# Mixer steps after quarters of a dense tile, early set-up loads, and block sums of the second channel weights on GpSimd

## The chip, the cores and the metric

The kernel runs on one core of a Trainium2 chip. A core has five engines that work at the same time and wait for one another by semaphores: TensorE (PE in the profile; its weight loads are PEld), VectorE (DVE), ScalarE (ACT), GpSimd (POOL) and SyncE (SP), which issues DMAs. The metric is device time in microseconds for one execution, the median of three runs. The profile is one more execution, taken with the hardware profiler.

## The reference

It is one layer of an encoder over 2048 tokens of width 1024, all in float32:

```
h = rmsnorm(x, norm_mix);  proj = h @ w_in
y_a = short_conv(...)       # gated convolution over 3 tokens
y_b = s5(...)               # complex diagonal state space, scan, GLU
y_c = sliding_window_attention(...)   # 4 query heads, 2 key heads, sinks
y_d = hgrn2(...)            # gated linear recurrence, 4 heads
x = x + rmsnorm_by_group([y_a, y_b, y_c, y_d]) @ w_out
x = x + square(relu(rmsnorm(x, norm_ffn) @ w_ff1)) @ w_ff2     # 1024 -> 4096 -> 1024
```

## The kernel before

**Precision.** A float32 operand is split into a high part (a copy in fp32r by ACT) and a low part (raw minus high, by DVE); a product is then three matmuls, high by high, high by low, low by high (`mm3`, L508). Every weight block is loaded raw (`wr`, by SP), split into `wh` (L105 or L1128) and `wl` (L111 or L1129), and used. This is the "dense" work.

**The mixer.** The tokens are worked in four blocks of 512. For each block, generators give the dense tiles: `attn_in` (4 tiles), `hgrn_in` (4), `conv_group` (6), `s5_in` (2), `hgrn_in2` (4). A dense tile (`proj_fm` or `tm_tile`) is 24 matmuls of 128x512 into one PSUM bank `mm`. Beside them run *tracks*: generators of the small work of the four groups (`attn`, `hgrn`, `conv_finish`, `s5_step`, and `s5_setup`, which makes the tables and operators of the state space once). `dense` (L1065) runs a generator of dense tiles, and after each of its yields calls `advance` (L1050), which adds each track's pace to its account and lets it go one step for every whole unit in it. `drain` runs what is left of a track to its end. A second generator can be given as `side`: `make_hT(b + 1)`, the normalised and transposed input of the next block, in PSUM bank `tr`, or `out_in`, the input of the output projection. After the mixer, `outp` is the output projection (L1024).

**The attention track** works on four tiles of 128 tokens for each block. For a tile: `norm` (squares, DVE and GpSimd), three transposes and their evacuation to `qT` and `kT` (L753 to L760), and for each of two key heads the scores, the softmax, the transposes of the probabilities (L810) and the products (L826).

**The set-up track** first issues eleven loads (L229 to L244), then transposes, exponentials and sines on [128, 8] tiles in many small DVE instructions (L223, among others, reads the loaded `ldt`), tables by doubling, and operators that go to DRAM. Its `yield`s come after pieces of this.

**The channel mixer.** Both matmuls are done in 2x2 blocks with seven products instead of eight. The first (`ff1`, L1276, all matmuls in `prod`, L1267) has two halves of the tokens (`hf`) with 16 steps `j` each, so 32 steps; a step is seven products of 12 matmuls. `prep_step` makes the sums of the input for half 0 ahead of the loop and for half 1 in steps 2, 5, 8 and 11 of half 0; the latter go to DRAM and come back by `from_dram` (L1210), called at step 0 of half 1 under high priority. The second matmul (L1397) needs block differences of `w_ff2`, which `w2_sums(k)` makes for k = 0 to 15, one in each step of half 1: two loads into `x_` and `y_`, four subtractions, two stores into `tt_d`. The tiles of `prep_step`, `from_dram`, `w2_sums` and the later `sr` loads share the tag `xt`, which has two buffers.

**Order.** Nobody writes the queues by hand. Each instruction has a priority, by default its place in the program; a block under `tc.high_priority()` is put ahead. A planner lays the instructions of each engine in a fixed order from priorities and its own estimate of when an instruction is ready; on the chip each engine then works through its queue in that order and waits where an operand is not there yet. So an instruction can stand in its queue far from its place in the program, and a wait holds everything behind it on that engine.

Of the kernel before, what the change touches and what calls it, by code (L numbers as in the profile page):

```python
# [59 lines left out]
def emit(ctx, tc, a):  # L60
# [150 lines left out]
    def s5_setup():  # L211
        with tc.tile_pool(name="st", bufs=1) as st:
# [31 lines left out]
            SY.dma_start(out=db.rearrange("p a b -> p (a b)"), in_=a["s5_d"].partition_broadcast(16))  # L244

            pt = psum_sx()
            PE.transpose(pt[:, 0:8], lam[:, 0, :], ident[0:8, 0:8])
# [269 lines left out]
    def proj_fm(c0):  # L517
        ws = fm_units(a["w_in"], c0)
        ps = psum_mm()
        for k in range(KD):  # L520
            wh, wl = ws[k // 4]
            mm3(ps, wh[:, k % 4, :], wl[:, k % 4, :], hh[:, k, :], hl[:, k, :], k == 0, k == KD - 1)
        return ps

# [3 lines left out]
    def tm_tile(ws, i):  # L528
        ps = psum_mm()
        sl = slice(i * P, (i + 1) * P)  # L530
        for k in range(KD):
            wh, wl = ws[k]
            mm3(ps, hh[:, k, sl], hl[:, k, sl], wh, wl, k == 0, k == KD - 1)
        return ps

# [3 lines left out]
    def conv_group(b):  # L539
        ya = []  # L540
        for ct in range(2):
            ph = proj_fm(ct * P)
            with tc.high_priority():
                z = mix.tile([P, TB + 2], F32, tag="cvz", name="cvz")
                S.activation(out=z[:, 2:], in_=ph, func=AF.Copy)
            yield
            pc = proj_fm(512 + ct * P)
            with tc.high_priority():
# [7 lines left out]
                st8["ztail", ct] = zp  # L556
            yield
            pb = proj_fm(256 + ct * P)
            with tc.high_priority():
# [6 lines left out]
            ya.append(ac)  # L566
            yield
        st8["ya", b] = ya
# [26 lines left out]
    def s5_in(b):  # L595
        for ct in range(2):
            ps = proj_fm(768 + ct * P)
# [5 lines left out]
            yield  # L603

# [96 lines left out]
    def attn_in(b):  # L701
        ws = tm_units(a["w_in"], 1024)
        lst = []
        for i in range(4):
            ti = b * 4 + i
            ps = tm_tile(ws, i)
# [6 lines left out]
            yield  # L713
        st8["attn", b] = lst

    def attn(b):
# [30 lines left out]

        nx = norm(0)
        yield
        for i in range(4):  # L750
            ti = b * 4 + i
            qn, va, vs_next, (va_prev, vs_prev) = nx
            pt = psum_mx()  # L753
            for c in range(3):
# [5 lines left out]
            V.tensor_scalar(out=kT[:, k0:k0 + P], in0=pt[:, 256:384], scalar1=kgain, scalar2=None, op0=ALU.mult)  # L760
            yield
            ya = mix.tile([P, GW], F32, tag="aty", name="aty")
            nks = [min(3, ti * 2 + e + 1) * 64 for e in range(2)]
            for kv in range(2):
# [24 lines left out]
                for e in range(2):  # L789
# [11 lines left out]
                    vvs.append(parts)  # L801
                if kv == 1 and i < 3:
                    nx = norm(i + 1)
# [12 lines left out]
                else:  # L816
                    S.activation(out=pTs[:, 0], in_=pT[:, 0:256].rearrange("p (e q) -> p e q", e=2), func=AF.Copy)
                    V.tensor_copy(out=pTs[0:64, 1], in_=pT[0:64, 256:512].rearrange("p (e q) -> p e q", e=2))
                yield
                for rp in range(2):  # L820
# [25 lines left out]
    def hgrn_in(b):  # L846
        mk = lambda nm, n: [mix.tile([P, 2, 256], F32, tag=nm, name=nm, bufs=n) for _ in range(2)]
        QP, KQ, Fg = mk("QP", 2), mk("KQ", 2), mk("Fg", 2)
        for ct in range(2):
            ps = proj_fm(1536 + ct * P)  # L850
# [3 lines left out]
            yield  # L854
            ps = proj_fm(1792 + ct * P)
            with tc.high_priority():
                for hf in range(2):
# [5 lines left out]
                                    op0=ALU.mult, op1=ALU.add)  # L863
            yield
        st8["hg", b] = (QP, KQ, Fg)

    def hgrn_in2(b):
        ws = tm_units(a["w_in"], 2048)
        vs, gs = [], []
        for i in range(4):  # L870
            ps = tm_tile(ws, i)
            v = mix.tile([P, GW], F32, tag="hv", name="hv", bufs=4)
# [6 lines left out]
            gs.append(g)  # L879
            yield  # L880
        st8["hv", b] = vs, gs
# [142 lines left out]
    def outp(b):  # L1024
        for nh in range(2):
            ns = slice(nh * 512, (nh + 1) * 512)
            ws = tm_units(a["w_out"], nh * 512)
            for i in range(4):
                ps = tm_tile(ws, i)
                xr = c1.tile([P, 512], F32, tag="xr", name="xr", bufs=2)  # L1030
                t0 = b * TB + i * P
                SY.dma_start(out=xr, in_=a["x"][t0:t0 + P, ns])
# [3 lines left out]
                yield  # L1036

# [8 lines left out]

    def track(gen, pace, key):
        tracks.append([gen, pace, 0.0, key])

    def advance():  # L1050
        for t_ in list(tracks):
            t_[2] += t_[1]
            while t_[2] >= 1.0:
                t_[2] -= 1.0
                if next(t_[0], "end") == "end":
                    tracks.remove(t_)
                    break

# [6 lines left out]
    def dense(g, side=None):  # L1065

        for _ in g:
            if side is not None:
                next(side, None)
            advance()  # L1070

    with first(-4000):
        run(make_hT(0))
    s5p = None
    for b in range(NB):
        dense(attn_in(b))
# [23 lines left out]
    for b in range(3):  # L1100
        g = outp(b)
        for _ in range(4):
            next(g)
# [118 lines left out]
    def w2_sums(k):  # L1222
        x_, y_ = (big.tile([P, D], F32, tag="xt", name="w2r", bufs=2) for _ in range(2))
        for h, t_ in enumerate((x_, y_)):
            SY.dma_start(out=t_, in_=a["w_ff2"][(2 * k + h) * P:(2 * k + h + 1) * P, :])
        b11, b12, b21, b22 = x_[:, 0:512], x_[:, 512:], y_[:, 0:512], y_[:, 512:]
        tsub(b11, b12, b11)
        tsub(b12, b22, b12)
        tsub(b22, b22, b11)
        tsub(b21, b21, b22)  # L1230
        for h, t_ in enumerate((x_, y_)):
            SY.dma_start(out=tt_d[h][k], in_=t_)

# [86 lines left out]
    for hf in range(2):  # L1320
        for j in range(NJ):
# [119 lines left out]
```

## Time and profile before

| | |
|---|---|
| median of 3 runs | 2346.17 us (2341.35 to 2346.51) |
| the profiled execution | 2343.7 us, its span 2341.6 us |
| mixer, with the output projection | 0 to about 1015 us of the span |
| first channel matmul | about 1019 to 1711 us |
| second channel matmul | about 1715 us to the end |
| mean granted TensorE clock | 0.987 |
| DMA | 381.35 MB, 163 GB/s over the span |

Stretches are read by the idle time of PE in them, and then by what ended that idle time. In a row of waits stand the engine and line that waited, what it waited for, the total in us, how often, and the longest. In a row of a queue stand the start, the time of the instruction, engine and line, the tiles written and read, and in brackets the idle time before it and its releaser.

### The profile page before, as it was taken

The page shows a single profiled execution, that of the slowest core. Times are in us where ns is not written, and L with a number is a line of the kernel's source. Part 1 is how long each engine was busy: PE and PEld are TensorE (multiplying, and loading weights), DVE is VectorE, ACT ScalarE, POOL GpSimd, SP SyncE. Part 2 cuts the span into 40 slices and gives each one's busy share as a digit, 9 for nine tenths or more (in the row PEclk, how much of TensorE's full clock was granted, in tenths as well). Part 3 has the DMA queues.
Part 4 walks back from the last instruction along what each step waited for, and adds up shares of the span by engine and source line. Part 5 has one row for each costly group of instructions (what it writes and reads, how often), then busy time and mean ns, then how long its engine had stood idle before and what let it go on. Part 6 is the DMA issues. An engine that isn't in the chain of part 4 may idle for free.

```text
span 2341.6 us, 32446 instructions
## 1 busy us (share of the span) xinstructions
PE 2227.5 (95%) x11460; PEld 1761.9 (75%) x11460; DVE 1433.2 (61%) x3008; ACT 949.8 (41%) x1902; POOL 163.2 (7%) x208
## 2 busy tenths in 40 slices
PE   7799999999999999989999999999999999999999
PEld 6577777777777777767777777777778888888887
DVE  5786786787677654676655666676653344344342
ACT  4234325435433433455555554544543233133121
POOL 0122212121211110000000000000000000000000
PEclk9899999999999999999999999999999999999999
DMA  6323333434432547636656577888674454355542
GB/s 182 92 78 97 104 102 118 118 101 125 124 111 85 163 155 224 216 129 193 194 158 191 173 222 255 273 266 267 204 238 151 155 192 140 118 190 180 183 148 99
DMA packets 393347, 381.35 MB, mean 163 GB/s; under 512 B 35968, under 2 KB 310496, under 8 KB 393184
## 3 DMA queue, kind: packets, MB, share of 16 engines
q1 hardware_dynamic: 393184, 379.27, 52.5%
q8 instruction: 90, 1.47, 0.3%
q14 instruction: 73, 0.60, 0.1%
HBM read 261.77 MB, written 116.40 MB: 161 GB/s over the span
## 4 chain that ended last, share of the span: by engine, by line
PE 67%; DVE 13%; DMA 9%; ACT 4%; issue 3%; POOL 2%; SPq 1%; DVEq 0%; POOLq 0%; ACTq 0%
PE mm L1397 26%; PE mm L1267 10%; PE mm L509 5%; PE mm L511 5%; PE mm L510 5%; PE hx L1267 5%; DMA w2r<-in_w_ff_dram 2%; DVE wl L111 2%; PE mx L1267 2%; DVE tp L1138 2%; PE hx L921 1%; DMA fxs<-x1d 1%; PE mx L826 1%; ACT wh L1128 1%; DVE w2r L1138 1%
## 5 line engine op out<-in xcount | busy, mean ns | idle before, releaser
L1397 PE MATMUL mm<-wh,st 128*128 128x512 f32 x1792 | 561.8, 394 | 1.4 <-ACT wh L1128 1.4
L1397 PEld LDWEIGHTS mm<-wh,st 128*128 128x128 f32 x1792 | 337.4, 188 | 80.0 <-ACT wh L1128 1.9
L1397 PE MATMUL mm<-wl,st 128*128 128x512 f32 x896 | 353.6, 395 | 0.2 <-DVE wl L1129 0.2
L1267 PE MATMUL mm<-tb,wh 128*128 128x512 f32 x1024 | 330.3, 403 | 24.5 <-ACT tp L1280 6.5
L1368 ACT ACTIVATE st<-sr 128x1024 fp32r<-128x1024 f32 x112 | 114.6, 1054 | 402.8 <-PE mm L1397 359.2
L1267 PEld LDWEIGHTS mm<-tb,wh 128*128 128x128 f32 x1024 | 189.6, 191 | 85.1 <-ACT tp L1286 14.7
L105 ACT ACTIVATE wh<-wr 128x512 fp32r<-128x512 f32 x224 | 138.6, 628 | 201.8 <-PE mm L510 163.0
L509 PE MATMUL mm<-wh,hh 128*128 128x512 f32 x512 | 208.3, 407 | 2.1 <-ACT hh L504 2.1
L1129 DVE TENSOR_TENSOR wl<-wr,wh 128x512 fp32r<-128x512 f32 x208 | 138.1, 688 | 113.6 <-ACT wh L1128 70.2
L1267 PE MATMUL mm<-tb,wl 128*128 128x512 f32 x512 | 204.5, 399 | 0.0
L511 PE MATMUL mm<-wh,hl 128*128 128x512 f32 x512 | 204.4, 399 | 0.0
L510 PE MATMUL mm<-wl,hh 128*128 128x512 f32 x512 | 204.0, 398 | 0.0
L1397 PEld LDWEIGHTS mm<-wl,st 128*128 128x128 f32 x896 | 168.4, 188 | 40.5 <-DVE wl L1129 0.5
L1369 DVE TENSOR_TENSOR st<-sr,st 128x1024 fp32r<-128x1024 f32 x112 | 133.9, 1222 | 94.8 <-ACT st L1368 94.6
L1267 PE MATMUL hx<-tb,wh 128*128 128x512 f32 x512 | 162.3, 397 | 8.4 <-ACT wh L1128 8.4
L111 DVE TENSOR_TENSOR wl<-wr,wh 128x512 fp32r<-128x512 f32 x224 | 151.3, 694 | 30.5 <-ACT wh L105 26.3
L509 PE MATMUL mm<-hh,wh 128*128 128x512 f32 x384 | 159.5, 415 | 0.0
L511 PE MATMUL mm<-hh,wl 128*128 128x512 f32 x384 | 154.9, 403 | 0.0
L510 PE MATMUL mm<-hl,wh 128*128 128x512 f32 x384 | 154.5, 402 | 0.0
L1128 ACT ACTIVATE wh<-wr 128x512 fp32r<-128x512 f32 x208 | 125.4, 625 | 64.6 <-PE mm L1267 28.1
L1138 DVE TENSOR_TENSOR tq<-mm,tq 128x512 f32<-128x512 f32 x32 | 22.1, 691 | 173.0 <-PE mm L1397 172.9
L1273 ACT ACTIVATE tp<-tp 128x512 f32<-128x512 f32 x96 | 60.5, 630 | 163.0 <-DVE tp L1138 156.2
(372 smaller groups left out, 3627.6 us busy)
## 6 DMA issues: line engine op xcount, KB each, us to landing
as<-tp SPq DMA_DIRECT2D x224, 256.0 KB, 2.8
sr<-as SPq DMA_DIRECT2D x112, 512.0 KB, 4.4
wr<-in_w_ff_dram SPq DMA_DIRECT2D x176, 256.0 KB, 3.8
wr<-in_w_in_dram SPq DMA_DIRECT2D x160, 256.0 KB, 3.1
wr<-in_w_out_dram SPq DMA_DIRECT2D x64, 256.0 KB, 4.1
w2r<-in_w_ff_dram SPq DMA_DIRECT2D x32, 512.0 KB, 4.6
tt<-w2r SPq DMA_DIRECT2D x32, 512.0 KB, 2.7
wr<-tt SPq DMA_DIRECT2D x64, 256.0 KB, 4.0
```

The costliest lines, as they stand in the source:

```text
L105: S.activation(out=hi, in_=raw, func=AF.Copy)
L111: (G if le == "p" else V).tensor_tensor(out=lo, in0=raw, in1=hi, op=ALU.subtract)
L509: PE.matmul(ps, lhsT=lh, rhs=rh, start=first, stop=False)
L510: PE.matmul(ps, lhsT=lh, rhs=rl, start=False, stop=False)
L511: PE.matmul(ps, lhsT=ll, rhs=rh, start=False, stop=last)
L1128: S.activation(out=h, in_=raw, func=AF.Copy)
L1129: V.tensor_tensor(out=l, in0=raw, in1=h, op=ALU.subtract)
L1138: V.tensor_tensor(out=o, in0=x, in1=y, op=op)
L1267: PE.matmul(ps, lhsT=(wh, wl)[lw][:, ks], rhs=b[lb][:, k, :], start=first and k == 0 and q == 0, stop=k == 3 and q == 2, skip_group_check= ...
L1368: S.activation(out=s_[:, 0, ks], in_=r, func=AF.Copy)
L1369: V.tensor_tensor(out=s_[:, 1, ks], in0=r, in1=s_[:, 0, ks], op=ALU.subtract)
L1397: PE.matmul(ps, lhsT=st_[:, ls, k, :], rhs=tu[i, k][lt], start=k == 0 and p_ == 0, stop=k == NJ - 1 and p_ == 2)
```

## The change

- A dense tile yields after its second, fourth and sixth of its eight groups of three matmuls too (so after each 6 of its 24 matmuls), and `True` at its end. `dense` advances the tracks at each of these, and `side` at the ends alone. `advance` lets a track go one step at most. The paces are given anew: attention 1.35 per tile to 0.29 per quarter, set-up 1.5 to 0.45, HGRN 1.25 to 0.34, conv 0.5 to 0.15, S5 1.0 to 0.34 in block 2 and 0.27 in block 3; tracks begin with something in their account. The first half of `outp` advances by quarters as well.
- `s5_setup` yields after its loads. It is run up to there ahead of the first dense tile, and becomes a track after `hgrn_in(0)` instead of after `attn_in(0)`.
- In the attention, the transposes for the next tile (`turn`) are issued with the second key head of the tile before, in PSUM bank `tr` instead of `mx`; `norm` of the next tile comes with the first key head instead of the second.
- `w2_sums` has its DMAs issued by GpSimd instead of SP and its subtractions done by GpSimd instead of DVE. It is called in steps 12 to 15 of half 0 and 2 to 13 of half 1, instead of 0 to 15 of half 1.

```diff
@@ s5_setup, after its loads
+            yield
             pt = psum_sx()
@@ proj_fm, and the same in tm_tile
             mm3(ps, wh[:, k % 4, :], wl[:, k % 4, :], hh[:, k, :], hl[:, k, :], k == 0, k == KD - 1)
+            if k in (1, 3, 5):
+                yield
         return ps
@@ conv_group, and the same in s5_in, attn_in, hgrn_in, hgrn_in2 and outp
-            ph = proj_fm(ct * P)
+            ph = yield from proj_fm(ct * P)
...
-            yield
+            yield True
@@ attn
-        nx = norm(0)
-        yield
-        for i in range(4):
-            ti = b * 4 + i
-            qn, va, vs_next, (va_prev, vs_prev) = nx
-            pt = psum_mx()
+        def turn(i, qn):
+            pt = psum_tr()
...
             V.tensor_scalar(out=kT[:, k0:k0 + P], in0=pt[:, 256:384], scalar1=kgain, scalar2=None, op0=ALU.mult)
-            yield
+            return qT
+
+        nx = norm(0)
+        yield
+        qT_next = turn(0, nx[0])
+        yield
+        for i in range(4):
+            ti = b * 4 + i
+            _, va, vs_next, (va_prev, vs_prev) = nx
+            qT = qT_next
...
-                if kv == 1 and i < 3:
+                if kv == 0 and i < 3:
                     nx = norm(i + 1)
                 yield
...
+                if kv == 1 and i < 3:
+                    qT_next = turn(i + 1, nx[0])
                 yield
@@ advance
             t_[2] += t_[1]
-            while t_[2] >= 1.0:
+            if t_[2] >= 1.0:
                 t_[2] -= 1.0
                 if next(t_[0], "end") == "end":
                     tracks.remove(t_)
-                    break
@@ dense
-        for _ in g:
-            if side is not None:
+        for end in g:
+            if end and side is not None:
                 next(side, None)
             advance()
@@ the blocks
+    setup = s5_setup()
+    next(setup)
     for b in range(NB):
         dense(attn_in(b))
         drain("hg")
-        track(attn(b), 1.35, "at")
-        if b == 0:
-            track(s5_setup(), 1.5, "set")
+        track(attn(b), 0.29, "at", 0.5)
         if b == 2:
...
-            track(s5_step(0), 1.0, "s5")
+            track(s5_step(0), 0.34, "s5", 0.3)
         if b == 3:
...
-            track(s5_step(1), 1.0, "s5")
+            track(s5_step(1), 0.27, "s5", 0.3)
         dense(hgrn_in(b))
-        track(hgrn(b), 1.25, "hg")
+        if b == 0:
+            track(setup, 0.45, "set", 0.3)
+        track(hgrn(b), 0.34, "hg", 0.9)
         dense(conv_group(b))
-        track(conv_finish(b), 0.5, "cv")
+        track(conv_finish(b), 0.15, "cv")
@@ the output projection
-        for _ in range(4):
+        for n in range(16):
             next(g)
             advance()
@@ w2_sums
-            SY.dma_start(out=t_, in_=a["w_ff2"][(2 * k + h) * P:(2 * k + h + 1) * P, :])
+            G.dma_start(out=t_, in_=a["w_ff2"][(2 * k + h) * P:(2 * k + h + 1) * P, :])
...
-        tsub(b11, b12, b11)
-        tsub(b12, b22, b12)
-        tsub(b22, b22, b11)
-        tsub(b21, b21, b22)
+        for o, p_, q_ in ((b11, b12, b11), (b12, b22, b12), (b22, b22, b11), (b21, b21, b22)):
+            G.tensor_tensor(out=o, in0=p_, in1=q_, op=ALU.subtract)
...
-            SY.dma_start(out=tt_d[h][k], in_=t_)
+            G.dma_start(out=tt_d[h][k], in_=t_)
@@ the loop over steps of the first channel matmul
-            if hf == 1:
-                w2_sums(j)
+            n = hf * NJ + j
+            if 12 <= n < 16 or 18 <= n < 30:
+                w2_sums(n - 12 if n < 16 else n - 14)
```

More of the change, by code (lines that the diff above doesn't have):

```diff
@@ L533, in tm_tile @@
             mm3(ps, hh[:, k, sl], hl[:, k, sl], wh, wl, k == 0, k == KD - 1)
+            if k in (1, 3, 5):
+                yield
         return ps
@@ L545, in conv_group @@
                 S.activation(out=z[:, 2:], in_=ph, func=AF.Copy)
-            yield
-            pc = proj_fm(512 + ct * P)
+            yield True
+            pc = yield from proj_fm(512 + ct * P)
             with tc.high_priority():
@@ L556, in conv_group @@
                 st8["ztail", ct] = zp
-            yield
-            pb = proj_fm(256 + ct * P)
+            yield True
+            pb = yield from proj_fm(256 + ct * P)
             with tc.high_priority():
@@ L566, in conv_group @@
             ya.append(ac)
-            yield
+            yield True
         st8["ya", b] = ya
@@ L596, in s5_in @@
         for ct in range(2):
-            ps = proj_fm(768 + ct * P)
+            ps = yield from proj_fm(768 + ct * P)
             with tc.high_priority():
@@ L602, in s5_in @@
             SY.dma_start(out=u_d[b // 2][ct * P:(ct + 1) * P, :, n0:n0 + 64], in_=us)
-            yield
+            yield True
     def s5_step(s):
@@ L705, in attn_in @@
             ti = b * 4 + i
-            ps = tm_tile(ws, i)
+            ps = yield from tm_tile(ws, i)
             qk = mix.tile([P, 384], F32, tag="qk", name="qk", bufs=4)
@@ L712, in attn_in @@
             lst.append((qk, va))
-            yield
+            yield True
         st8["attn", b] = lst
@@ L746, in norm @@
             return qn, va, vs_next, prev
-        nx = norm(0)
-        yield
-        for i in range(4):
-            ti = b * 4 + i
-            qn, va, vs_next, (va_prev, vs_prev) = nx
-            pt = psum_mx()
+        def turn(i, qn):
+            pt = psum_tr()
             for c in range(3):
@@ L760, in attn @@
             V.tensor_scalar(out=kT[:, k0:k0 + P], in0=pt[:, 256:384], scalar1=kgain, scalar2=None, op0=ALU.mult)
-            yield
+            return qT
+        nx = norm(0)
+        yield
+        qT_next = turn(0, nx[0])
+        yield
+        for i in range(4):
+            ti = b * 4 + i
+            _, va, vs_next, (va_prev, vs_prev) = nx
+            qT = qT_next
             ya = mix.tile([P, GW], F32, tag="aty", name="aty")
@@ L849, in hgrn_in @@
         for ct in range(2):
-            ps = proj_fm(1536 + ct * P)
+            ps = yield from proj_fm(1536 + ct * P)
             with tc.high_priority():
@@ L853, in hgrn_in @@
                     S.activation(out=QP[hf][:, ct], in_=ps[:, hf * 256:(hf + 1) * 256], func=AF.Copy)
-            yield
-            ps = proj_fm(1792 + ct * P)
+            yield True
+            ps = yield from proj_fm(1792 + ct * P)
             with tc.high_priority():
@@ L863, in hgrn_in @@
                                     op0=ALU.mult, op1=ALU.add)
-            yield
+            yield True
         st8["hg", b] = (QP, KQ, Fg)
@@ L870, in hgrn_in2 @@
         for i in range(4):
-            ps = tm_tile(ws, i)
+            ps = yield from tm_tile(ws, i)
             v = mix.tile([P, GW], F32, tag="hv", name="hv", bufs=4)
@@ L879, in hgrn_in2 @@
             gs.append(g)
-            yield
+            yield True
         st8["hv", b] = vs, gs
@@ L1028, in outp @@
             for i in range(4):
-                ps = tm_tile(ws, i)
+                ps = yield from tm_tile(ws, i)
                 xr = c1.tile([P, 512], F32, tag="xr", name="xr", bufs=2)
@@ L1035, in outp @@
                 SY.dma_start(out=x1_d[b][i * P:(i + 1) * P, ns], in_=xr)
-                yield
+                yield True
     def run(g):
@@ L1045, in emit, with track @@
     tracks = []
-    def track(gen, pace, key):
-        tracks.append([gen, pace, 0.0, key])
+    def track(gen, pace, key, start=0.0):
+        tracks.append([gen, pace, start, key])
     def advance():
```

## The prediction

> **What bounds the kernel now.** I read the page first, then the table of stretches, then the waits of each engine inside the stretches, then the queues in order of time. TensorE (PE) is the bound nearly everywhere: the page gives it 95% of the span. The stretches show where it isn't. Columns: stretch, its length, busy time (and instructions) of PE, weight loads, DVE, ACT, POOL, granted clock, DMA share, GB/s.
>
> ```profile
> span 2341.6 us, 32446 instructions
> ...
> PE 2227.5 (95%) x11460; PEld 1761.9 (75%) x11460; DVE 1433.2 (61%) x3008; ACT 949.8 (41%) x1902; POOL 163.2 (7%) x208
> ...
> 45.00:65.00 20.00, 14.49 (x67) 11.15 (x65) 6.96 (x26) 5.46 (x13) 0.00 (x0) 0.93 0.51 119
> 65.00:245.00 180.00, 163.53 (x1125) 127.24 (x1126) 141.90 (x488) 69.56 (x190) 34.81 (x41) 0.94 0.33 96
> 245.00:430.00 185.00, 179.14 (x1220) 139.28 (x1219) 136.49 (x355) 73.03 (x198) 38.70 (x44) 1.00 0.37 104
> 430.00:605.00 175.00, 168.47 (x1224) 132.68 (x1223) 138.11 (x406) 70.25 (x199) 32.25 (x39) 1.00 0.39 111
> 605.00:790.00 185.00, 175.27 (x1165) 136.76 (x1164) 139.01 (x389) 74.84 (x214) 31.64 (x40) 0.97 0.40 116
> 790.00:965.00 175.00, 166.82 (x852) 135.26 (x853) 96.51 (x215) 63.26 (x143) 13.53 (x20) 0.99 0.59 193
> 1730.00:2341.00 611.00, 607.62 (x2615) 491.92 (x2614) 244.65 (x293) 166.94 (x212) 0.00 (x0) 1.00 0.48 158
> ```
>
> The last row is the second channel matmul, which has no idle PE to win and which the change leaves alone. The four rows from 65 to 790 are about one mixer block each. PE is idle for 16.5, 5.9, 6.5 and 9.7 us in them, and 5.5 us in the 20 us ahead. So block 0 (45 to 245) idles 22.0 us against a mean of 7.4 in the others. The cause stands in the waits of PE and in the queues of SP and DVE.
>
> ```profile
> PE mx L770 <- DVE kT L760: 8.6, 1, 8.6
> PE mx L810 <- DVE apr L790: 7.2, 4, 2.9
> ...
> 32.41 0.94 SPq L199 DMA_DIRECT2D wgr<-in_s_w_glu_dram  x2
> 33.40 0.52 SPq L727 DMA_DIRECT2D vs<-va  x1
> 33.96 0.52 SPq L229 DMA_DIRECT2D lam<-in_s_lam_re_dram  x1
> 43.11 4.14 SPq L102 DMA_DIRECT2D wr<-in_w_in_dram  x6
> ...
> 49.54 1.80 SPq L240 DMA_DIRECT2D ldt<-in_s_log_dt_dram  x2
> ...
> 61.73 0.17 DVE L223 TENSOR_SCALAR t<-ldt 128x8 f32<-128x8 f32 x1 [11.41 <-DMA ldt<-in_s_log_dt_dram]
> ```
>
> DVE stands 11.41 us at L223 for the load of `ldt`, and the attention's `kT` (L760) is queued behind it, so PE stands 8.6 us. The clock then falls:
>
> ```profile
> 62.40:72.60 10.20, 4.01 (x11) 3.21 (x12) 8.83 (x47) 3.88 (x8) 1.34 (x1) 0.50 0.63 209
> 79.40:89.60 10.20, 9.86 (x34) 7.23 (x35) 5.48 (x28) 2.20 (x10) 0.00 (x0) 0.50 0.18 52
> ```
>
> In those two stretches PE worked 4.01 + 9.86 us at half clock, of which half, 6.9 us, is lost. [...]
>
> The second place is the first channel matmul (L1267). Its 32 steps (16 for each half of the tokens) need 84 matmuls each. Rows of L1267 alone: stretch, length, PE busy, weight loads, clock, DMA.
>
> ```profile
> 1280.90:1320.70 39.80, 39.58 (x169) 31.20 (x170) 1.00 0.67 197
> 1413.10:1687.80 274.70, 262.99 (x1093) 203.69 (x1092) 0.99 0.81 258
> ```
>
> Two quiet steps of the first half take 39.8 us, 19.9 each. Thirteen steps of the second half, beside `w2_sums`, take 274.7, 21.13 each: 16.0 us more than thirteen quiet ones. From 1405 to 1715 the waits of DVE and SP name `w2_sums`:
>
> ```profile
> DVE w2r L1138 <- DMA w2r<-in_w_ff_dram: 31.7, 18, 3.7
> SPq L1232 <- DVE w2r L1138: 53.4, 26, 5.2
> SPq L1225 <- DMA tt<-w2r: 17.8, 12, 4.1
> ACT wh L1128 <- DVE tp L1138: 46.2, 14, 5.7
> ```
>
> **The change, part by part.** The sum is made against the profiled execution's own time, 2343.7 us (its span is 2341.6); the median of the runs shown, 2346.17, is 2.5 above.
>
> *Set-up loads and set-up track.* The eleven DMAs of the set-up are written ahead of the first dense tile, its arithmetic now starts after `hgrn_in(0)` instead of after `attn_in(0)`. At most this wins block 0's extra idle (22.0 - 7.4 = 14.6) and the half clock (6.9), 21.5 us. At least it wins nothing: in the queue the set-up loads already follow the last constant (L199, then one `vs` copy, then L229), so there is hardly an earlier place, and `ldt` comes 16 us after L229 because weights' loads (six in the L102 row) are put in between. What the move does remove is the crowd behind the wait: DVE was busy 8.83 of 10.20 us after it, mostly with set-up instructions, and the second wait (L810) and second half clock come from that. The order in the queues is not program order (priority decides, and what is ready fills gaps: `outp(0)`'s first load starts at 67 us), so L223 may still be put ahead of its data. The first `vs` copy now stands behind the set-up loads, eleven issues of about half a us (the L229 row); only the attention's products wait for it, later, and dense matmuls cover that. I take half, **11 us**.
>
> ```profile
> 67.31 0.97 SPq L1032 DMA_DIRECT2D xr<-in_x_dram  x2
> ```
>
> *Quarters.* No instruction is added. A track step now comes after a quarter of a dense tile (6 matmuls) instead of after 24, and never two at once. Attention goes from 1.35 steps a tile to 0.29 a quarter, 1.16 a tile, with 19 steps instead of 22, so it ends at the same place; HGRN 1.25 to 1.36; set-up 1.5 to 1.8; S5 1.0 to 1.36 in block 2. That last one matters: 25 steps at 1.0 a tile over 20 tiles left five for `drain("s5")`, run in one lump; at 1.36 none is left. The attention's transposes of the next tile go ahead of the last product, so `kT` is early. What can go is idle time in blocks 1 to 3, 5.9 + 6.5 + 9.7 = 22.1 us; the largest wait of 430 to 605 is only 2.3 us in three (the L810 row below), and much of the rest is dependence that stays. Against it: `turn` moves from the two `mx` banks to the single `tr` bank, which `make_hT` and `conv_finish` use too. If each of the 16 turns waited for one evacuation of that bank (0.60 us, the row below), 10 us would be lost. Between 22 won and 10 lost I take **7 us** won, a third of the idle, because the waits are many and short. The stretch 790 to 965 keeps its `out_in` at tile ends (the L1016 row): 0; half of its 5.8 us either way goes into the range.
>
> ```profile
> PE mx L810 <- DVE apr L790: 2.3, 3, 1.4
> PE tr L1016 <- DVE hl L1021: 5.8, 6, 2.0
> ...
> L504 ACT ACTIVATE hh<-tr 128x512 fp32r<-128x512 f32 x8 | 4.8, 600 | 1.3 <-PE tr L500 1.3
> ```
>
> *`w2_sums` on GpSimd.* From DVE go 64 subtractions of 0.691 us, 44.2, and the waits of 31.7; from SP's queue go 64 DMAs and the three waits on them (53.4 and 17.8 are the largest), behind which the weights' loads stood; ACT's weight splits (`wh`) stood 46.2 us behind DVE. GpSimd gets 64 subtractions and 64 DMAs; no pow is left for it after step 11, so nothing is queued behind them. The nearest GpSimd row is L904, 128x512 with two inputs; the two rows of `w2r` stand ahead of it:
>
> ```profile
> L1138 DVE TENSOR_TENSOR w2r<-w2r x64: 680/691/694, 1399.8 to 1653.7; 128x512 f32<-128x512 f32 x64
> DMA to landing us min/median/max: 2.6/3.6/6.7
> ...
> L904 POOL TENSOR_TENSOR hacc<-ident,he x16: 1037/1090/1557, 97.6 to 694.3; 128x512 f32<-128x512 f32 x16
> L939 POOL TENSOR_TENSOR KQ<-KQ,bp x48: 616/706/1667, 121.7 to 801.7; 128x256 f32<-128x256 f32 x48
> L842 DVE SCALAR_TENSOR_TENSOR goy<-aty,gorsc,g_grp x16: 475/485/1075, 106.5 to 787.4; 128x256 f32<-128x256 f32 x16
> ```
>
> Four of 1.09 are 4.4 us of a 19.9 us step, so GpSimd is not short of time. But the maxima beside the minima (1667 against 616 on GpSimd, 1075 against 475 on DVE) show that the two engines stop each other at times. The bound: every GpSimd subtraction stops DVE for its whole length, 64 x 1.09 = 69.8 us, against 44.2 + 31.7 = 75.9 freed. So at worst nearly all is given back, and at best the 16.0 us of the thirteen steps are won. DVE is two thirds busy there, so about half the meetings should hurt: I take **8 us**. [...]
>
> No row shows a DMA issued by GpSimd. The bounds: as cheap as SP's (the L1032 row: 0.97 us for two); at most, a step's four together cost one more landing, 6.7 us at worst for `w2r`. I take the first, since four DMAs a step fit in the time GpSimd has left; both ends are in rival 3. [...]
>
> Sum: 11 + 7 + 8 = 26; 2343.7 - 26 = 2317.7, and with 2.5 to the median **2320**.
>
> **The rivals.**
>
> 1. *The orders do not matter, because the loads are not early and the tracks already filled the gaps.* For it: L229 stands right behind the constants, and work is placed by readiness. Against it: the lump of five S5 steps and the double steps of attention and HGRN go, whatever else stays. Then only the 8 us of `w2_sums` remain: 2346 - 8 = 2338.
>
> 2. *The two engines exclude each other.* Then 69.8 of 75.9 us come back and `w2_sums` wins about 0; 2346 - 18 = 2328. Against it: only the maxima, not the medians, are long in the rows above.
>
> 3. *Slower: `from_dram` comes late.* `w2_sums(0..3)` now stand at steps 12 to 15, ahead of `from_dram`, and share the two `xt` buffers with it.
>
> ```profile
> L1216 SPq DMA_DIRECT2D tr<-tb x14: 320/338/555, 1277.5 to 1392.3; - x14
> L1218 DVE TENSOR_TENSOR tb<-tr,tb x14: 1218/1226/1227, 1333.8 to 1397.5; 128x1024 fp32r<-128x1024 f32 x14
> tt<-w2r SPq DMA_DIRECT2D x32, 512.0 KB, 2.7
> ```
>
> The last row is the store of a sum. Seven operands pass two buffers, each pair about a landing (5 us) and splits (2 us), 49 us. They end now at 1398.7. If four sums of t us each start at 1277.5, they end at 1277.5 + 4t + 49, later than now once t is over 18.0. By the rows t is 3.6 + 4 x 1.09 + a store of 2.7 = 10.7, and with every maximum 6.7 + 4 x 1.56 + 2.7 = 15.6; with 6.7 more for GpSimd's DMAs it is 22.3, and PE waits 17 us. With no gain in the mixer and 8 us of the later sums kept: 2346 + 17 - 8 = 2355.
>
> 4. *The mixer gets worse*: the 10 us of the `tr` bank, no set-up gain, half of `w2_sums`' 8: 2352.
>
> **How the numbers follow.** Forecast (2300 to 2337): 0.55. Rival 1: 0.16, rival 2: 0.12, rival 3: 0.10, rival 4: 0.07. The likeliest time is 2320. All upper bounds together, 21.5 + 22.1 + 16, would be 2286, which I hold for very unlikely; the range goes from 2298 to rival 3's 2354. No change means within 0.3%, 7 us, about what a measurement tells. Faster by more: the forecast, rival 2 and half of rival 1 (its 2338 lies on the edge), less 0.02 for sizes, 0.73. Within: the other half and 0.05 of rival 4, 0.13. Slower: rival 3, the rest of rival 4 and 0.02 for sizes, 0.14.
>
> **What would show it.** Right: DVE's wait on `ldt` short or gone, no half clock from 62 to 90, and PE idle in block 0 near 10; idle in blocks 1 to 3 near 15 together; steps of the second half near 20.5 us, DVE's wait on `w2r` gone. Wrong: L223 still at 61 us; PE waiting on `tr` for the attention's transposes; DVE's tensor_tensor median well over 0.69 beside GpSimd; `from_dram`'s splits ending after 1400.

## The result, and the profile after

The changed kernel takes **2378.73 us** in the median (2370.92 to 2381.45, 4 runs), the kernel before beside it 2346.34. The ratio is 1.013 (95% interval 1.0102 to 1.0158): 1.3% slower, where 2320 was predicted. The profiled execution of the changed kernel took 2370.92 us.

These lines are from the profile page of the changed kernel: the span, then the busy time of each engine. PE has exactly the busy time it had before; what was added is idle PE. POOL went from 163 to 293 us.

```profile
span 2369.2 us, 32494 instructions
...
PE 2227.5 (94%) x11460; PEld 1761.7 (74%) x11460; DVE 1429.9 (60%) x2944; ACT 952.5 (40%) x1902; POOL 293.1 (12%) x336
```

The mixer's stretches, in the columns of the first table of the prediction:

```profile
45.00:65.00 20.00, 12.39 (x54) 9.92 (x53) 7.04 (x23) 6.08 (x13) 1.22 (x1) 0.88 0.57 140
65.00:245.00 180.00, 168.09 (x1140) 129.33 (x1140) 142.82 (x486) 69.73 (x189) 37.27 (x42) 0.93 0.31 92
245.00:430.00 185.00, 177.00 (x1206) 137.46 (x1204) 136.89 (x354) 72.97 (x196) 36.18 (x43) 0.99 0.36 102
430.00:605.00 175.00, 164.60 (x1186) 126.77 (x1185) 141.22 (x414) 72.83 (x209) 33.72 (x41) 1.00 0.42 120
605.00:790.00 185.00, 178.56 (x1291) 140.51 (x1290) 145.52 (x402) 75.54 (x216) 34.93 (x42) 1.00 0.38 111
```

Block 0 idles 7.6 + 11.9 = 19.5 us (before 22.0), blocks 1 to 3 idle 8.0 + 10.4 + 6.4 = 24.8 (before 22.1). So there is no less idle time. The waits of 45 to 65 show that the wait of block 0 is still there:

```profile
DVE t L223 <- DMA ldt<-in_s_log_dt_dram: 10.3, 1, 10.3
...
PE mx L780 <- DVE kT L761: 7.6, 1, 7.6
```

The loss lies in the first channel matmul. Its matmuls alone (L1267 before, L1278 after): the whole, then step 14, steps 15 to 23, step 24, and steps 25 to 30. First the kernel before, then the changed one.

```profile
1019.40:1711.30 691.90, 648.01 (x2688) 501.38 (x2687) 0.99 0.69 212
1320.70:1344.60 23.90, 20.36 (x85) 15.32 (x83) 1.00 0.53 158
1344.60:1540.20 195.60, 184.32 (x757) 141.59 (x758) 0.98 0.80 251
1540.20:1564.50 24.30, 21.45 (x86) 16.51 (x85) 0.93 0.90 284
1564.50:1687.80 123.30, 119.34 (x505) 93.22 (x504) 1.00 0.78 247
```

```profile
1012.60:1739.70 727.10, 654.95 (x2688) 509.19 (x2687) 0.96 0.66 202
1317.10:1350.60 33.50, 23.28 (x86) 17.49 (x84) 0.80 0.73 229
1350.60:1561.80 211.20, 189.23 (x757) 145.86 (x758) 0.95 0.78 243
1561.80:1598.80 37.00, 21.98 (x85) 17.00 (x84) 0.82 0.77 247
1598.80:1716.30 117.50, 117.50 (x506) 93.73 (x505) 1.00 0.51 150
```

It is 35.2 us longer: steps 14 and 24 lose 9.6 and 12.7, the nine between them 15.6, and the six after the last sum, now at 19.6 each without any idle time, win 5.8. The rest is step 13 (19.57 us before, 23.63 after) and trifles. The second channel matmul is unchanged (630 us).

*The two long steps.* The waits of SP's queue, from 1310 to 1350 and from 1550 to 1600:

```profile
SPq L1229 <- DMA w2r<-in_w_ff_dram: 11.2, 1, 11.2
SPq L1229 <- DMA tt<-w2r: 9.4, 2, 8.2
```
```profile
SPq L1379 <- DMA w2r<-in_w_ff_dram: 21.8, 1, 21.8
SPq L1379 <- DMA tt<-w2r: 9.2, 2, 7.8
```

L1229 is the first `tr` load of `from_dram`, L1379 the first `sr` load of the second channel matmul. Both need one of the two `xt` buffers, which GpSimd's sums hold. Behind them, in the same queue, stand weights' loads in step 14 and, in step 24, the stores of `as` that set free the `tp` tiles. In the same two windows DVE, ACT and PE wait for those:

```profile
DVE tp L1151 <- DMA wr<-in_w_ff_dram: 7.7, 1, 7.7
...
PE hx L1278 <- ACT wh L1141: 6.6, 1, 6.6
```
```profile
ACT tp L1284 <- DMA as<-tp: 15.0, 1, 15.0
...
PE mm L1278 <- ACT tp L1284: 14.1, 1, 14.1
```

In these stalls the clock falls to half, for 13.7 and 13.6 us (the clock is the column before the last two):

```profile
1333.30:1347.00 13.70, 6.90 (x15) 4.96 (x16) 8.47 (x12) 4.25 (x8) 0.00 (x0) 0.50 1.06 328
...
1575.70:1589.30 13.60, 4.33 (x10) 3.47 (x11) 1.39 (x2) 1.23 (x2) 2.49 (x4) 0.50 0.89 281
```

*DVE beside GpSimd.* Groups of 1260 to 1600 (count, busy time, mean ns of one, then idle time before):

```profile
L1241 POOL TENSOR_TENSOR w2r<-w2r 128x512 f32<-128x512 f32 x64 | 91.0, 1421 | 61.0 <-DMA w2r<-in_w_ff_dram 59.4
...
L1142 DVE TENSOR_TENSOR wl<-tp,wh 128x512 fp32r<-128x512 f32 x56 | 43.9, 844 | 1.1 <-ACT wh L1141 1.1
L1151 DVE TENSOR_TENSOR tp<-tp 128x512 f32<-128x512 f32 x56 | 43.6, 814 | 30.0 <-ACT tp L1285 29.4
...
L1151 DVE TENSOR_TENSOR tp<-mx,tp 128x512 f32<-128x512 f32 x14 | 9.5, 680 | 0.0
L1151 DVE TENSOR_TENSOR tp<-hx,tp 128x512 f32<-128x512 f32 x13 | 9.0, 691 | 15.2 <-PE hx L1278 15.2
```

DVE's subtractions with two inputs in SBUF (`wl`, `tp<-tp`) went from 0.69 us to a mean of 0.81 to 0.84; those with one input in PSUM (`mx`, `hx`) stayed at 0.68 to 0.69. Single ones took up to 2.26 us; 33 were lengthened, by some 31.5 us together, and each of the 33 overlaps a subtraction of GpSimd. Fourteen subtractions with a PSUM input overlap GpSimd's too, and none of them took over 0.69 us.

### The profile page after: what moved, and what is told of

It is laid out like the page before. It is cut to its first block, busy times and chain, and to the rows that moved or that the text cites. A ratio compares the mean times of both kernels' runs of the same rounds, so it can differ in the third digit from the quotient of the medians.

```text
span 2369.2 us, 32494 instructions
## 1 busy us (share of the span) xinstructions
PE 2227.5 (94%) x11460; PEld 1761.7 (74%) x11460; DVE 1429.9 (60%) x2944; ACT 952.5 (40%) x1902; POOL 293.1 (12%) x336
## 4 chain that ended last, share of the span: by engine, by line
PE 60%; DMA 13%; DVE 12%; issue 6%; POOL 5%; ACT 4%; SPq 0%; POOLq 0%; DVEq 0%; ACTq 0%
PE mm L1409 25%; PE mm L1278 8%; PE mm L510 5%; PE mm L511 4%; PE mm L512 4%; DMA w2r<-in_w_ff_dram 4%; PE hx L1278 4%; POOL w2r L1241 3%; DMA tt<-w2r 2%; DVE wl L111 2%; PE mx L1278 2%; DMA fxs<-x1d 1%; PE hx L933 1%; DMA xt<-in_x_dram 1%; PE mx L838 1%
## 5 line engine op out<-in xcount | busy, mean ns | idle before, releaser
L1278 PE MATMUL mm<-tb,wh 128*128 128x512 f32 x1024 | 335.1, 408 | 39.6 <-ACT tp L1284 17.7
L1278 PEld LDWEIGHTS mm<-tb,wh 128*128 128x128 f32 x1024 | 193.8, 194 | 99.8 <-ACT tp L1284 23.4
L1142 DVE TENSOR_TENSOR wl<-wr,wh 128x512 fp32r<-128x512 f32 x208 | 145.0, 720 | 146.0 <-ACT wh L1141 76.6
L1278 PE MATMUL mm<-tb,wl 128*128 128x512 f32 x512 | 206.6, 404 | 0.0
L1278 PE MATMUL hx<-tb,wh 128*128 128x512 f32 x512 | 163.5, 399 | 11.6 <-ACT wh L1141 11.6
L111 DVE TENSOR_TENSOR wl<-wr,wh 128x512 fp32r<-128x512 f32 x224 | 151.2, 691 | 29.0 <-ACT wh L105 28.3
L1151 DVE TENSOR_TENSOR tp<-tp 128x512 f32<-128x512 f32 x136 | 96.1, 741 | 51.1 <-ACT tp L1285 49.2
```

What stands on the lines that cost most here:

```text
L111: (G if le == "p" else V).tensor_tensor(out=lo, in0=raw, in1=hi, op=ALU.subtract)
L1142: V.tensor_tensor(out=l, in0=raw, in1=h, op=ALU.subtract)
L1151: V.tensor_tensor(out=o, in0=x, in1=y, op=op)
L1278: PE.matmul(ps, lhsT=(wh, wl)[lw][:, ks], rhs=b[lb][:, k, :], start=first and k == 0 and q == 0, stop=k == 3 and q == 2, skip_group_check= ...
```

## The experiments

Three theories follow from these rows: **Q**, SP's queue stands behind the `xt` buffers; **L**, DVE and GpSimd stop each other; **M**, the mixer's new order matters. A fourth came with the first results: **P**, pace, that on GpSimd's queue nothing keeps the sums from running ahead and crowding the weights' work. Every ratio is to the kernel before on the same chip, with its 95% interval. The column "x clock" is the mean over a kernel's runs of span times mean granted clock, an estimate of what its time would be without half clock. It is a rough one: where PE waits anyway, half clock costs nothing (in the two stalls above PE worked 6.90 of 13.7 us and 4.33 of 13.6), so it comes out too low for kernels with such stalls. The kernel before has 2311.8 to 2313.4 in the five groups of runs, at clock 0.986 to 0.987.

| kernel | mixer | sums: buffers, arithmetic, DMAs, steps | median us | ratio | clock, x clock |
|---|---|---|---|---|---|
| changed | new | xt, GpSimd, GpSimd, 12-15 and 18-29 | 2378.7 | 1.0130 [1.0102, 1.0158] | .977, 2321.1 |
| mixer_only | new | as before | 2345.0 | 0.9999 [0.9984, 1.0014] | .984, 2303.4 |
| own_buffers | new | own, GpSimd, GpSimd | 2360.5 | 1.0064 [1.0044, 1.0084] | .980, 2310.2 |
| xt_dve_sub | new | xt, DVE, GpSimd | 2376.5 | 1.0136 [1.0119, 1.0153] | .978, 2320.8 |
| own_dve_sub | new | own, DVE, GpSimd | 2374.6 | 1.0118 [1.0097, 1.0140] | .976, 2314.0 |
| own_sp_dve | new | own, DVE, SP, 16-31 | 2342.0 | 0.9995 [0.9973, 1.0018] | .984, 2302.7 |
| own_sp_steps | new | own, DVE, SP, 12-15 and 18-29 | 2345.8 | 1.0001 [0.9982, 1.0020] | .982, 2303.0 |
| own_paced | new | own, GpSimd, GpSimd, held to 13-28 | 2336.6 | 0.9964 [0.9944, 0.9985] | .983, 2295.1 |
| own_dve_paced | new | own, DVE, GpSimd, held to 13-28 | 2347.4 | 0.9988 [0.9965, 1.0010] | .984, 2306.2 |
| xt_paced | new | xt, GpSimd, GpSimd, held to 13-28 | 2351.3 | 1.0021 [1.0003, 1.0039] | .982, 2307.7 |
| ff2_sums | new | second channel matmul, DVE, SP | 2386.7 | 1.0177 [1.0143, 1.0211] | .973, 2318.4 |
| ldt_first | new, `ldt` loaded first | as before | 2339.4 | 0.9979 [0.9957, 1.0001] | .984, 2302.4 |
| setup_held | new, loads held back | as before | 2345.1 | 0.9996 [0.9977, 1.0015] | .984, 2305.5 |
| best | new, loads held back | own, GpSimd, held to 12, 13, 17-30 | 2333.2 | 0.9937 [0.9908, 0.9965] | .985, 2295.8 |
| before_paced | before | as best | 2332.9 | 0.9940 [0.9915, 0.9964] | .988, 2304.0 |
| setup_only | before, set-up early | as best | 2337.5 | 0.9964 [0.9945, 0.9983] | .985, 2301.0 |
| quarters_only | quarters, set-up as before | as best | 2329.6 | 0.9942 [0.9918, 0.9966] | .985, 2294.2 |

**One part at a time: mixer, buffers, engine.** In `mixer_only`, `w2_sums` and its call are those of the kernel before. The others keep the changed kernel's calls. The own buffers are one `gain` and two `xr` tiles, idle by then; `xt_dve_sub` keeps `xt` and has only the last edit:

```
     def w2_sums(k):
-        x_, y_ = (big.tile([P, D], F32, tag="xt", name="w2r", bufs=2) for _ in range(2))
+        x_ = c1.tile([P, D], F32, tag="gain", name="w2r")
+        b21, b22 = (c1.tile([P, 512], F32, tag="xr", name="w2y", bufs=2) for _ in range(2))
...
-            G.tensor_tensor(out=o, in0=p_, in1=q_, op=ALU.subtract)
+            V.tensor_tensor(out=o, in0=p_, in1=q_, op=ALU.subtract)      # the two ..._dve_sub
```

> The mixer part of the change alone; the block sums as before (SyncE's DMAs, DVE's subtractions, one sum at each step of the second half). Theory Q (SyncE's queue stands behind the two `xt` buffers that GpSimd holds) and theory L (GpSimd and DVE stop each other) both put the whole loss in the first channel matmul, so both expect its 727.2 us to go back to about 692, and the whole time to about 2340 us: 2346.3 less the 6.8 us by which the first channel matmul started earlier in the changed kernel (1012.6 against 1019.4). Theory M (the mixer's new order also harms the first channel matmul, or the 6.8 us are an accident of one profile) expects 2346 or more.

> The changed kernel with GpSimd's sums in buffers of their own (one of `gain`, two of `xr`, all idle by then) instead of the two `xt` buffers. Theory Q expects the two long steps (33.5 and 37.1 us, with 13.7 us of half clock each) to go back to 20 to 21 us, and the late weights' loads of steps 13 to 23 with them: some 30 us won, about 2345 us. Theory L expects that only the order of the waits changes: GpSimd still lengthens DVE's subtractions (33 of them, 31.5 us in all), 2370 us or more.

> The changed kernel with the 64 subtractions of the sums back on DVE; GpSimd still issues their DMAs, and the tiles stay in the two `xt` buffers. Theory L expects DVE's maxima back at 0.69 us, and with them most of the loss: about 2345 us. Theory Q expects that the two `xt` buffers are still held in front of SyncE's queue, each sum by some 5 us less (four times 0.69 on DVE instead of four times 1.30 on GpSimd): the two long steps remain at about 30 us, and the time is 2360 us or more.

> Both taken away: the sums in buffers of their own, their subtractions on DVE, their DMAs issued by GpSimd. Both theories expect a first channel matmul of about 685 us (32 steps of 19.6 to 20, and 45 us of the half clocks and the second half's operands), 2335 us in all. If it is not under 2350, a third cause is left: GpSimd's way of issuing DMAs, or where the sums stand.

`mixer_only` is at the time before: the whole loss is the sums', and the mixer part wins nothing (the first channel matmul starts at 1020.4 us there, so the 6.8 us by which it started earlier in the changed kernel were an accident of one profile). By the ratios own buffers bring back 0.66% (15 us) of the 1.30% (31 us), DVE's arithmetic alone nothing, and both together 0.12% (3 us). So Q explains half; and L's effect is there (with DVE's arithmetic no subtraction is lengthened, their means in `own_dve_sub` being 0.68 to 0.69 us; with GpSimd's some 42.5 us are added in `own_buffers`), but taking it away does not bring the time back, since DVE then stands itself for the sums' loads. Neither theory explains the last kernel. Its waits from 1241 to 1488:

```profile
DVE w2r L1244 <- DMA w2r<-in_w_ff_dram: 27.9, 12, 5.5
...
DVE w2r L1244 <- DMA w2y<-in_w_ff_dram: 18.7, 9, 5.3
```

The first channel matmul's rows of `own_dve_sub` show where the time goes, steps 10 to 18 full of stalls at clock 0.90, then steps 19 to 30 with none:

```profile
1241.80:1488.80 247.00, 200.37 (x757) 151.81 (x756) 0.90 0.88 278
1488.80:1723.60 234.80, 234.80 (x1009) 187.35 (x1008) 1.00 0.50 148
```

Nine steps of 27.4 us, then twelve of 19.57: all sums ran between 1228 and 1480 us, some 16 us each and from step 9 on, though they are written at 12 to 29. Nothing on GpSimd's queue holds them to their steps, and DVE stands 46.6 us for their loads (the two rows of waits).

**Queue or pace.** The same sums with SP's DMAs, at the steps 16 to 31 and then at the changed kernel's; and GpSimd's DMAs with a hold:

```
+        G.tensor_copy(out=x_[:, 0:1], in_=held[:, 0:1])     # held: the step's last split weight, u[6][0]
         G.dma_start(out=x_, in_=a["w_ff2"][r_ - P:r_, :])
...
+            if 13 <= n < 29:
+                w2_sums(n - 13, u[6][0])
```

The load has to wait for the copy into its buffer, and the copy for a weight that is split about when its step starts.

> The mixer of the changed kernel, the sums as in the kernel before (SyncE's DMAs, DVE's subtractions, one at each step of the second half), but in the idle `gain` and `xr` buffers instead of `xt`. It differs from the run with own buffers and DVE's subtractions (2374.6 us) in the queue that issues the DMAs and in the steps where the sums stand. Theory P (pace: what throttles the sums is SyncE's queue, where each sum's loads stand behind the weights' loads; on GpSimd's queue nothing holds them, so they crowd into 8 to 12 steps and everything on DVE comes late) expects 2340 to 2350, as with the mixer part alone. Theory B (the shared `xt` buffers are what throttles the sums to one a step, whoever issues) expects 2365 or more.

> Own buffers, DVE's subtractions, SyncE's DMAs, with the sums written at the changed kernel's steps (12 to 15 and 18 to 29) instead of 16 to 31. Between the run on SyncE's queue (2342.0 us) and the one on GpSimd's (2374.6) both the queue and the steps differed. Theory P (GpSimd's queue is what lets sums and weights' loads run over each other: weights' loads took 7.5 us to land there, 4.3 on SyncE's) expects 2340 to 2350 here. Theory S (the earlier steps make the sums more urgent than the weights' splits of the steps after them) expects 2365 or more.

> GpSimd's sums in their own buffers, each held back to its step (13 to 28) by a copy of one column from that step's last split weight into the buffer that the load then overwrites. Theory P expects that the crowding goes, and with it most of the 18 us that own buffers still lost: 2345 or less. Theory L (DVE's two-input subtractions are lengthened by GpSimd's, 42.5 us in all with own buffers) expects the same 40 us of lengthening, spread over 16 steps of 19.6 us, and some 10 us of it on PE: 2355 or more.

> As the paced run with own buffers (2336.6 us), but with the 64 subtractions on DVE; GpSimd issues the DMAs, each sum held to its step. It differs from the run with DVE's subtractions and no pace (2374.6) in the pace alone. Theory P expects most of those 32 us back, 2335 to 2350. Theory D (DVE stands in its own order for sums' loads that GpSimd issues, whatever their pace: 46.6 us of such waits without pace) expects 2360 or more: then it was GpSimd's arithmetic, which keeps those waits off DVE, that made the paced run good.

> The changed kernel with one thing added: each sum is held back to its step (13 to 28), as in the paced run, but in the two `xt` buffers as they were. With the paced run (own buffers, 2336.6 us), the run of own buffers without pace (2360.5) and the changed kernel (neither, 2378.7) it completes a square. Theory P says that the pace alone wins most: the two long steps go, since no sum holds `xt` when `from_dram` or the second channel matmul asks for it except those of steps 13 to 16, about 2345. Theory Q says that the shared buffers still put SyncE's queue behind GpSimd, and the loads of a held sum now keep them for longer: 2355 or more.

The two on SP's queue are at the time before, whatever the steps. `own_sp_steps` differs from `own_dve_sub` in the queue alone: the queue, not the position, costs 1.2% (27 to 29 us). But SP's queue does not hold the sums to their steps either. Here are the first subtractions of the 16 sums (shortest, median and longest in ns, then the first and last start in us), in `own_sp_steps` and in `own_dve_sub`:

```profile
L1244 DVE TENSOR_TENSOR w2r<-w2r x16: 683/690/694, 1232.5 to 1524.3; 128x512 f32<-128x512 f32 x16
```
```profile
L1244 DVE TENSOR_TENSOR w2r<-w2r x16: 682/691/694, 1232.2 to 1472.5; 128x512 f32<-128x512 f32 x16
```

On both queues the sums start in step 9, three steps ahead of their place. On SP's they come every 19.5 us in the mean, as long as a quiet step, and on GpSimd's every 16.0. The weights' loads show another difference. First `own_sp_steps`, then `own_dve_sub`, issues of 1238 to 1512, last column the median us to landing:

```profile
wr<-in_w_ff_dram SPq DMA_DIRECT2D x48, 256.0 KB, 4.1
```
```profile
wr<-in_w_ff_dram SPq DMA_DIRECT2D x41, 256.0 KB, 6.8
```

In `own_sp_steps` SP issues a sum's loads in line with the weights' loads; in `own_dve_sub` GpSimd issues them beside SP's, and the weights land later, 6.8 us after their issue in the median instead of 4.1. The later landing alone is not the loss: in `own_paced`, with GpSimd's DMAs as well, it is 6.6 us while the sums run (1305 to 1647), and that kernel loses nothing (0.9964). While the sums run, PE waits 29 us in `own_dve_sub` for weights that ACT splits, and 9.5 in `own_sp_steps`; DVE, which stands ahead of ACT there, waits 46.6 and 34.8 us for sums' loads. Which part of the crowding costs how much is not shown.

Holding the sums to their steps gives 1.3% back with DVE's arithmetic (1.0118 to 0.9988, 30 us) and 1.0% with GpSimd's (1.0064 to 0.9964, 23 us). `xt_paced` completes the square of shared or own buffers, without and with pace: 1.0130 and 1.0064, 1.0021 and 0.9964. Each wins by itself, 1.0 to 1.1% for the pace, 0.6 to 0.7% for the buffers. So P and Q hold. (`xt_paced`, at 2351, lies between the 2345 that P alone expected and the 2355 of Q. The paced kernels are also written at other steps, 13 to 28, but on SP's queue the steps did not matter.) Theory D, that DVE's order is what matters whatever the pace, is wrong.

L is smaller than expected. In `own_paced` the lengthening is 23 us, half of what `own_buffers` has, and its steps 17 to 30 are near the quiet 19.57:

```profile
1403.70:1686.50 282.80, 278.25 (x1177) 217.05 (x1176) 1.00 0.77 238
```

282.8 for 14 steps is 20.2 each: PE is idle for at most 4.6 us in them, so with the sums spread the lengthening costs PE little. With the pace, GpSimd's arithmetic is no worse than DVE's (0.9964 against 0.9988; the intervals overlap).

**The sums elsewhere.** Written into the first eleven tiles of the second channel matmul, on DVE, in the output tiles' buffers (`tq`):

> The mixer of the changed kernel, the 16 sums on DVE with SyncE's DMAs, moved out of the first channel matmul into the first 11 tiles of the second (87 us each 8), in the output tiles' buffers. In every theory the first channel matmul then has no sums beside it: its first 14 steps as they are (300 us), 17 of 19.57 us, 3.9 at the end and about 10 for the second half's operands, 647 us instead of 692 to 727. If the second channel matmul hides 44 us of subtractions in the 120 us of its first 11 tiles, where DVE is 40% busy, the time is about 2345 - 45 = 2300. If the crowd only moves (a new wait on the weights of the third product, or on the splits), 2320 to 2345.

The first channel matmul is 670 us (647 were expected), so all sums together cost some 22 of its 692 us before. But PE then stands 60 us in one piece. Waits of 1800 to 1880:

```profile
PE mm L1411 <- DVE tq L1151: 59.8, 1, 59.8
DVE tq L1151 <- DMA tq<-in_w_ff_dram: 41.3, 15, 6.6
```

The first `finish` takes its `tq` tile behind the sums in the rotation, and PE's PSUM bank waits for that `finish`. The crowd moved, as the second case of the expectation had it, only worse: a shared rotation of buffers again.

**The set-up and the mixer's parts.** `ldt_first` moves the two `ldt` loads ahead of `lam`; `setup_held` holds all eleven loads by one-column copies of block 0's last `va`; `setup_only` and `quarters_only` take one half of the mixer part each, with paced sums.

> The mixer part alone (2345.0 us), with the two loads of `ldt` issued first of the set-up's loads instead of last but one: at about 34.5 us instead of 48.5 and 50.9. They land some 9 us after the second issue. DVE's wait of 10.3 us at L223 should go; if PE's wait of 7.6 us on `kT` and the half clock after it go with it, block 0 gains 8 to 11 us, about 2336. If the attention's products stand for something else instead, the time stays within 2340 to 2349.

> The mixer part alone (2345.0 us), with the eleven loads of the set-up held back behind block 0's last `va` (some 60 us), by copies of a few columns that GpSimd makes into the buffers that the loads then overwrite. The set-up's arithmetic still starts after `hgrn_in(0)`. If it is the crowd of small loads and set-up arithmetic in block 0 that costs the waits on `kT` (7.6 us) and `apr` and the half clock, these go, and the time is about 2332. If the attention's first products wait for other things, or DVE now stands for `ldt` later, the time stays within 2338 to 2350.

With `ldt` first, DVE doesn't wait for it, but the weights come later, and two rows of DVE's timeline show 4.7 us of waiting for those instead:

```profile
51.30 0.69 DVE L111 TENSOR_TENSOR wl<-wr,wh 128x512 fp32r<-128x512 f32 x1 [4.68 <-ACT wh L105]
...
52.80 0.16 DVE L223 TENSOR_SCALAR t<-ldt 128x8 f32<-128x8 f32 x1
```

With the loads held back, the wait on `ldt` moves with them and is as long as before, and PE waits for `apr` instead of `kT`:

```profile
PE mx L826 <- DVE apr L806: 14.0, 2, 10.6
...
DVE t L223 <- DMA ldt<-in_s_log_dt_dram: 10.2, 1, 10.2
```

So with the loads early or late, as the change and this kernel have them, the set-up's first instruction stands in DVE's order some 10 us before its data. Without that wait some 5 us may be won (0.9979 against 0.9999, but the intervals overlap).

> The kernel before with the paced sums of the last kernel (2332.9 us), and of the change's mixer part the set-up alone: loads ahead of the first dense tile, arithmetic after `hgrn_in(0)` at 1.8 steps a tile. The prediction gave this 11 us. If that holds and the quarters take it back, about 2322. If the set-up is worth nothing by itself, 2330 to 2336. Start of the first channel matmul less half of the half-clock time was 999 and 1000 in the two profiles of the mixer before and 991 to 994 in the twelve of the changed mixer: if the set-up makes that difference, it is near 992 here.

> The paced sums, and of the change's mixer part the quarters and the attention's turn alone: the set-up's loads and arithmetic start after `attn_in(0)` as before, at 0.375 steps a quarter. The prediction gave this 7 us. If that holds, about 2326. If quarters win idle time and lose it in half clock (37 to 68 us of half clock ahead of the first channel matmul in the twelve profiles of the changed mixer, 41 and 20 in the two of the mixer before), 2330 to 2340, with the start of the first channel matmul less half of its half-clock time near 992, and more half clock than 41 us.

Beside `before_paced` (2332.9), the set-up alone gives 2337.5 and the quarters alone 2329.6; the ratios 0.9940, 0.9964 and 0.9942 overlap. The last column of the table suggests more: by it the quarters win 9.8 us (2304.0 to 2294.2) and the set-up 3.0, and the mixer part as a whole 8.4 (2311.8 to 2303.4). But the mean clock falls, from 0.987 to 0.984 in `mixer_only`, 0.3% of 2340 us or some 8 us. So by this column the gain is paid back in half clock. This is worked out from the mean clock and not shown by a run of its own; which stalls bring the half clock was not tried.

**The kernels that beat both.**

> Put together: the changed kernel's mixer with the held set-up loads, and GpSimd's sums in their own buffers, paced over the steps 12, 13 and 17 to 30, so that none stands at the steps 14 to 16 where `from_dram` makes the second half's operands (in the paced run these three took 79.2 us, without sums 71.3). By the sum of the parts: 2336.6, less 8 for those steps and less what the held set-up gives (0 to 13): 2316 to 2329.

> The mixer of the kernel before, unchanged, with GpSimd's sums in their own buffers, paced over the steps 12, 13 and 17 to 30. If the change's mixer part is worth nothing (its run alone gave 0.9999), this is the paced run less the 8 us of the steps 14 to 16: about 2329. If the change's mixer gains a little that its run alone could not show, this is 5 or more above it.

Both came out at 0.994, some 13 us under the kernel before and 45 under the changed one: what wins is GpSimd's sums in buffers of their own, and paced. That it also helps to keep them away from the steps of `from_dram` is not shown: `own_paced` without that has 0.9964, and the intervals overlap. The expectations (2316 to 2329, and 2329) were a little low: the held set-up gave nothing, and the three steps 14 to 16 took 73.6 and 69.9 us in these profiles, near the 71.3 hoped for.

## Why the prediction was wrong, point by point

- **`w2_sums` on GpSimd: -8 predicted, +35 in the trace of the first channel matmul, and 1.3% (31 us) by the ratios of the changed kernel and `mixer_only`.** This is the step that failed, at its sentence "I take the first, since four DMAs a step fit in the time GpSimd has left". It priced the move of the DMAs by their issue alone, and an issue did cost little (0.54 us). It put at nothing what SP's queue did by its order: there the sums' loads stood in line with the weights'. On GpSimd's queue they ran ahead (a sum every 16.0 us instead of 19.5) and beside them (weights landing in 6.8 us instead of 4.1), which costs 1.2% between `own_sp_steps` and `own_dve_sub`, and the sums held the two buffers that SP's queue needed. Of the changed kernel's 1.3%, the pace alone gives back 1.1% and buffers of their own 0.7%; both together give back all of it and 0.4% more. The freed waits were real in part: DVE's on `w2r` and SP's on DVE's subtractions (53.4 us) are gone. SP's on the stores `tt` only moved, from 17.8 us ahead of the sums' loads to 9.4 and 9.2 ahead of the `tr` and `sr` loads.
- **Rival 3 had the right place and the wrong price.** A sum took 13 to 16 us, under the 18.0 from which it was to decide, and `from_dram` ended only 9 us later (1408 against 1399). Its seven operands took 82 us from the first load, at 1326, where the rival had 49. PE did not wait for `from_dram` but for the weights' loads *behind* its waiting load in SP's queue. The same trap at step 24, for the second channel matmul's `sr`, was not seen at all.
- **Rival 2** (mutual stops): the stops are there, some 31.5 us, a little under half of the bound of 69.8, and GpSimd's subtraction is longer than the row taken for it (1.30 us instead of 1.09). But they don't decide: paced, GpSimd's arithmetic is no worse than DVE's.
- **Set-up, -11 predicted, 0 measured** for the mixer part as a whole. The doubt in the prediction ("L223 may still be put ahead of its data") was the truth, and its mark of failure, L223 still at 61 us, came (60.67). It should have been the value taken.
- **Quarters, -7 predicted:** they were worth 10 us by the column "x clock" and nothing that the ratios show in time. Idle in blocks 1 to 3 was to be near 15 and was 24.8. The `tr` bank did not turn out a bottleneck: no wait of an attention transpose on it is among the large ones. That the quarters would come with a lower clock (0.985 in the mean in `quarters_only`, 0.988 in `before_paced`) was not among the rivals.
- **Rival 1** was right for the mixer (0), and wrong for the sums it left at -8.

## What to carry over

A queue that looks like an obstacle may be what keeps the transfers on it out of each other's way (here the weights landed in 4.1 us with the sums' loads on their queue, in 6.8 with them on another): when DMAs move from a busy queue to an idle one, ask what will hold them back there, and if nothing does, hold them with a dependence. A buffer shared between queues ties them: the cost is not the late transfer but everything issued behind the one that waits (SP stood 11.2 and 21.8 us, and PE 6.6 and 14.1 us for what came behind). And read a kernel's idle PE together with its granted clock, since a gain in one can be lost in the other: the column "x clock" puts the mixer part's gain at 8.4 us, an estimate, while the mean clock went from 0.987 to 0.984 and the time stayed.

## What was not expected of the hardware

The granted clock varies from run to run for one and the same program: the twelve runs of `mixer_only` have a mean clock between 0.980 and 0.988, and the time roughly goes with it (2347.3 us at 0.980, 2336.9 at 0.988). The same mixer, instruction for instruction on PE, took the first channel matmul's start from 1012.6 us (profile of the changed kernel) to 1025.2 (`own_paced`), with 37.5 and 68.3 us of half clock ahead of it. These runs do not show the cause. Short stalls can be followed by half clock, though not always: in `mixer_only` a wait of 2.0 us that ends at 296.7 is followed by 3.4 us at half clock (timeline of PE, then that stretch), but in the profile of the changed kernel a wait of 2.0 us that ends at 1726.65 is not (the same two rows for it, below).

```profile
296.72 0.41 PE L820 MATMUL mx<-ident,apr 128*128 128x128 f32 x2 [1.97 <-DVE apr L800]
```
```profile
298.80:302.20 3.40, 3.40 (x10) 2.62 (x9) 1.94 (x5) 0.95 (x2) 0.00 (x0) 0.50 0.04 10
```
```profile
1726.65 0.73 PE L1278 MATMUL mm<-tb,wh 128*128 128x512 f32 x2 [1.97 <-ACT tp L1291]
```
```profile
1726.65:1740.00 13.35, 11.71 (x50) 9.26 (x51) 6.99 (x11) 7.66 (x13) 0.00 (x0) 1.00 0.74 216
```
